# Gate and up of the last two token blocks as seven products of combined quarters, in passes of one block

## The chip, the core and the metric

The kernel runs on one core of one Trainium2 chip. The metric is the device time of one execution in microseconds (us), the median of several runs. The engines are named as in the profile: PE (matrix products; PEld is its loading of stationary operands), DVE and ACT (element-wise work; both read the PSUM banks), POOL (element-wise work on SBUF only), SP (which issues the DMAs here).

## The reference

One transformer block on 2048 tokens of width 1024, in float32: a normalisation, mixers (attention, gated linear attention, pooling), an output projection, and a gated feed-forward part. The change concerns the last part:

```python
hn = rms_norm(h, ffn_norm_g[l])
ff = jax.nn.silu(jnp.einsum('bsd,df->bsf', hn, w_gate[l])) * jnp.einsum('bsd,df->bsf', hn, w_up[l])
h = h + jnp.einsum('bsf,fd->bsd', ff, w_down[l])
```

The width inside is 2816, that is 22 tiles of 128.

## The kernel before

Tokens are handled in four blocks of 512 (`BLK`). All matrix products use float32r operands, and each number is carried as a sum of two such parts, H and L, so that a product a*b takes three matmuls, H·H, H·L and L·H. Splitting a tile is a cast to H on ACT and a subtraction on POOL or DVE for L.

The first phase (P1) projects the inputs; attention runs beside it and beside the first half of the second phase. The second phase (P2) is the output projection and the feed-forward part. It goes in passes over the weights: block 0, block 1, then blocks 2 and 3 together (`PASSES`). A pass walks through 11 groups of two hidden tiles (`GS`):

- `gate_up` makes for one hidden tile and one block the gate and the up product, each into one PSUM bank: `tile24` has 8 row tiles times 3 matmuls of 128x128 by 128x512 (L1119 to L1121).
- `ch_ff` is the side chain behind it: DVE takes both banks out with the row scale (L1136, L1138), ACT forms the sigmoid in four steps (L1140 to L1144, with one DVE step L1143 between), DVE multiplies (L1145, L1146), ACT casts to H (L1150), DVE forms L (L1151).
- `down` work: for each of the 8 output tiles one bank takes 6 matmuls (L133, from `mm`), which need H and L of both hidden tiles; DVE adds the bank to the residual (L1157).

Weights come one tile of 128x1024 at a time: SP loads it into a raw buffer, `wprep` casts it on ACT (L451) and subtracts on POOL (L452) into a buffer of `wring`. In the last pass each prepared weight serves two blocks, and there are five weight buffers and four pairs for H and L.

The order on each engine is set when the program is built: side chains are Python generators that are advanced at every `tick()` as far as their buffers allow, and a scheduler then places the instructions by its own estimate. On the chip every engine works through its own list in that order and waits at semaphores.

Of the kernel before, what the change touches and what calls it, by code (L numbers as in the profile page):

```python
# [17 lines left out]
P = 128  # L18
S = 2048
D = 1024  # L20
KT = D // P
# [19 lines left out]
class Ring:  # L41
    """Buffers handed out in turn. A buffer comes back once its last reader is in the program."""
# [13 lines left out]
class Region:  # L56
    """A phase's memory: a pool of single buffers."""
# [30 lines left out]
def body(nc, tc, V, G, ACT, PE, DMA, A, banks, dram):  # L88
    side, rside = [], []
    rate = [0.0, 0.0]  # L90
    def spawn(g):
        """Put a chain into the program as far as its buffers allow."""
        if g is not None:
            side.append(g)
            advance([g], side)
# [18 lines left out]
    def force(g):  # L114
        """Run an acquisition to its end, letting the side chains go on."""
# [19 lines left out]
    # ------------------------------------------------------------- memory  # L135
# [3 lines left out]
    # ------------------------------------------------------------- constants  # L139
# [24 lines left out]
    # ------------------------------------------------------------- DRAM scratch  # L164
# [8 lines left out]
    # ============================================================== P1  # L173
# [18 lines left out]
    class Chain:  # L192
        """Buffers of a normalisation: the two parts of the squares, ln, the result, a bank."""
# [4 lines left out]
    def meansq(sq, ones, n, c):  # L198
        """Mean of squares over the partitions of a group: a bank."""
# [10 lines left out]
    def rsq(ms, n, c):  # L210
        """-2 / sqrt(ms + eps): one Newton step on exp(-ln/2)."""
# [13 lines left out]
    # ---- normalised input of a block  # L225
# [67 lines left out]
    # ---- side chains of the projection tiles  # L293
# [81 lines left out]
    def ch_v(c, b, j, bank):  # L375
        """v of one token tile, in natural layout, split in two parts."""
# [45 lines left out]
    # ---- weights  # L422
# [11 lines left out]
    PASSES = [[0], [1], [2, 3]]  # L434
    for ps in range(len(PASSES)):
        pieces += [(("o", ps, d), None, A["w_o"][d], 0) for d in range(KT)]
        for g0 in range(0, NF, GS):
            for fi in range(g0, g0 + GS):
                pieces.append((("g", ps, fi), None, A["w_g"][fi], 0))
                pieces.append((("u", ps, fi), None, A["w_u"][fi], 0))  # L440
            for fi in range(g0, g0 + GS):
                pieces.append((("d", ps, fi), None, A["w_d"][fi], 0))
    wst = dict(dma=0, prep=0)
# [24 lines left out]
    def pump():  # L468
        """Issue the loads and splits that have room."""
        while rawring.free and wst["dma"] < len(pieces):  # L470
# [3 lines left out]
            m = KT * P if n in (0, P) else 4 * n  # L474
# [3 lines left out]
        if wring.free and wst["prep"] < wst["dma"]:  # L478
# [845 lines left out]
```

## Time and profile before

| | us |
|---|---|
| median of three runs | 2682.47 |
| lowest and highest of them | 2677.68, 2683.40 |
| span of the profiled execution, first to last instruction | 2678.9 |
| PE busy in it | 2569.5 |
| DVE busy | 1786.7 |
| ACT busy | 1179.8 |
| POOL busy | 930.5 |

The profiled execution has no time of its own beside its span. The span lies 3.6 us under the median of the runs and between their ends, so what lies around it is inside the spread of the runs. Busy times of PE count overlapping matmuls once; the time of a stretch is better read from the distance of instruction starts.

### The profile page before, as it was taken

The page shows a single profiled execution, that of the slowest core. Times are in us where ns is not written, and L with a number is a line of the kernel's source. Part 1 is how long each engine was busy: PE and PEld are TensorE (multiplying, and loading weights), DVE is VectorE, ACT ScalarE, POOL GpSimd, SP SyncE. Part 2 cuts the span into 40 slices and gives each one's busy share as a digit, 9 for nine tenths or more (in the row PEclk, how much of TensorE's full clock was granted, in tenths as well). Part 3 has the DMA queues.
Part 4 walks back from the last instruction along what each step waited for, and adds up shares of the span by engine and source line. Part 5 has one row for each costly group of instructions (what it writes and reads, how often), then busy time and mean ns, then how long its engine had stood idle before and what let it go on. Part 6 is the DMA issues. An engine that isn't in the chain of part 4 may idle for free.

```text
span 2678.9 us, 34710 instructions
## 1 busy us (share of the span) xinstructions
PE 2569.5 (96%) x12480; PEld 2118.0 (79%) x12480; DVE 1786.7 (67%) x3676; ACT 1179.8 (44%) x2205; POOL 930.5 (35%) x607
## 2 busy tenths in 40 slices
PE   7999889989999999999999999999999999999999
PEld 5887778868777877888778887787888888888887
DVE  7769886689677778778767767676364444444444
ACT  3555545357655535445544544444332222222222
POOL 4336432355733333333533333332522222222220
PEclk8999999989999999999999999999999999999999
DMA  5333645335543333346434342425211111111111
GB/s 165 122 115 112 182 144 158 114 103 182 172 122 118 118 101 112 105 124 212 122 102 117 105 121 80 138 74 178 94 44 48 48 48 47 48 48 47 48 47 63
DMA packets 145882, 284.44 MB, mean 106 GB/s; under 512 B 15292, under 2 KB 59885, under 8 KB 145709
## 3 DMA queue, kind: packets, MB, share of 16 engines
q1 hardware_dynamic: 145420, 282.20, 33.5%
q8 instruction: 98, 1.61, 0.3%
q14 instruction: 76, 0.61, 0.1%
q10 hardware_dynamic: 288, 0.02, 0.0%
HBM read 230.91 MB, written 51.25 MB: 105 GB/s over the span
## 4 chain that ended last, share of the span: by engine, by line
PE 49%; DVE 3%; ACT 1%; DMA 1%; issue 0%; POOL 0%; SPq 0%; DVEq 0%; ACTq 0%
PE bk L133 17%; PE bk L1119 10%; PE bk L1121 10%; PE bk L1120 10%; PE bk L878 1%; DVE c L1146 1%; DMA c<-mix 1%; DVE at L853 0%; DVE at L833 0%; ACT at L845 0%; DVE c L1073 0%; DMA mix<-at 0%; DVE c L1145 0%; DVE c L1138 0%; DVE c L1143 0%
## 5 line engine op out<-in xcount | busy, mean ns | idle before, releaser
L1119 PE MATMUL bk<-c,c 128*128 128x512 f32 x1136 | 450.8, 398 | 4.0 <-DVE c L217 2.4
L1120 PE MATMUL bk<-c,c 128*128 128x512 f32 x1136 | 451.0, 397 | 2.3 <-DVE c L1102 2.0
L1121 PE MATMUL bk<-c,c 128*128 128x512 f32 x1136 | 450.6, 397 | 0.7 <-POOL c L452 0.7
L452 POOL TENSOR_TENSOR c<-c,c 128x1024 fp32r<-128x1024 f32 x105 | 262.2, 2498 | 487.7 <-ACT c L451 438.9
L133 PE MATMUL bk<-p,c 128*128 128x512 f32 x1184 | 322.5, 397 | 12.2 <-DVE p L217 3.9
L133 PEld LDWEIGHTS bk<-p,c 128*128 128x128 f32 x1184 | 217.8, 189 | 59.6 <-DVE c L1138 4.8
L1119 PEld LDWEIGHTS bk<-c,c 128*128 128x128 f32 x1136 | 213.4, 188 | 53.6 <-DVE c L217 2.6
L1120 PEld LDWEIGHTS bk<-c,c 128*128 128x128 f32 x1136 | 213.6, 188 | 52.5 <-DVE c L1102 3.4
L1121 PEld LDWEIGHTS bk<-c,c 128*128 128x128 f32 x1136 | 213.5, 188 | 49.4 <-POOL c L452 0.9
L845 ACT ACTIVATE at<-at,at 128x1024 f32<-128x1024 f32 (+4 forms) x192 | 171.6, 896 | 115.3 <-DVE at L842 114.8
L833 DVE TENSOR_SCALAR_CACHE_REDUCE at<-bk 128x512 f32<-128x512 f32 (+3 forms) x304 | 153.6, 518 | 92.1 <-PE bk L133 91.4
L451 ACT CAST c<-c 128x1024 fp32r<-128x1024 f32 x105 | 110.1, 1048 | 232.8 <-PE bk L133 116.0
L1157 DVE TENSOR_TENSOR p<-p,bk 128x512 f32<-128x512 f32 x264 | 176.3, 682 | 49.7 <-PE bk L133 48.3
L998 PE MATMUL bk<-c,c 128*128 128x512 f32 x448 | 184.8, 414 | 20.1 <-ACT c L462 10.5
L452 POOL TENSOR_TENSOR c<-p,c 128x1024 fp32r<-128x1024 f32 x51 | 124.9, 2449 | 209.2 <-ACT c L451 209.2
L999 PE MATMUL bk<-c,c 128*128 128x512 f32 x448 | 184.7, 412 | 5.5 <-DVE c L250 5.5
L133 PE MATMUL bk<-c,at 128*128 128x512 f32 (+4 forms) x704 | 176.1, 349 | 11.0 <-DVE at L833 3.8
L1000 PE MATMUL bk<-c,c 128*128 128x512 f32 x448 | 183.0, 408 | 0.1
L133 PE MATMUL bk<-c,c 128*128 128x256 f32 (+1 forms) x1152 | 152.4, 286 | 7.5 <-DVE p L393 3.6
L1143 DVE SCALAR_TENSOR_TENSOR c<-c,c 128x512 f32<-128x512 f32 x88 | 81.8, 930 | 114.2 <-ACT c L1142 114.1
L133 PEld LDWEIGHTS bk<-c,c 128*128 128x128 f32 x1152 | 145.9, 190 | 11.2 <-DVE p L393 4.7
L133 PEld LDWEIGHTS bk<-c,at 128*128 128x128 f32 x704 | 121.1, 191 | 35.8 <-DVE at L833 5.4
(238 smaller groups left out, 5384.1 us busy)
## 6 DMA issues: line engine op xcount, KB each, us to landing
c<-w_g SPq DMA_DIRECT2D x44, 512.0 KB, 3.3
c<-w_u SPq DMA_DIRECT2D x44, 512.0 KB, 3.4
c<-w_d SPq DMA_DIRECT2D x44, 512.0 KB, 3.3
c<-kd SPq DMA_DIRECT2D x72, 256.0 KB, 4.6
c<-vd SPq DMA_DIRECT2D x72, 256.0 KB, 3.3
c<-xT SPq DMA_DIRECT2D x64, 256.0 KB, 3.4
at<-qd SPq DMA_DIRECT2D x64, 256.0 KB, 4.1
c<-w_e SPq DMA_DIRECT2D x28, 512.0 KB, 3.6
```

The lines of the kernel that those rows point to most:

```text
L133: PE.matmul(out, l, r, start=start and i == 0, stop=stop and i == n - 1)
L451: ACT.copy(wH, raw[:, :1024])
L452: G.tensor_tensor(wL, raw[:, :1024], f(wH), op=ALU.subtract)
L833: V.tensor_scalar(p[:, c0:c0 + far], pt[:, :far], 1.0, None, op0=ALU.mult, op1=ALU.max, accum_out=mx[:, nx:nx + 1])
L845: ACT.activation(p[:, c0:c1], p[:, c0:c1], AF.Exp, bias=nmx, accum_out=u.z[:, i, m, k:k + 1])
L998: PE.matmul(bank, wH[:, kt, :], hH[:, kt, :], start=st, stop=False)
L999: PE.matmul(bank, wH[:, kt, :], hL[:, kt, :], start=False, stop=False)
L1000: PE.matmul(bank, wL[:, kt, :], hH[:, kt, :], start=False, stop=sp)
L1119: PE.matmul(bank, wH[:, kt, :], H[:, kt, :], start=st, stop=False)
L1120: PE.matmul(bank, wH[:, kt, :], L[:, kt, :], start=False, stop=False)
L1121: PE.matmul(bank, wL[:, kt, :], H[:, kt, :], start=False, stop=sp)
L1157: V.tensor_tensor(h2[q][d], h2[q][d], bank, op=ALU.add)
```

## The change

The gate and up products of blocks 2 and 3 are made with 7 instead of 8 sub-products, in Winograd's form. For two hidden tiles at once the weight (1024 rows by 256 columns) is cut in quarters A11, A12, A21, A22, and the normalised block (1024 by 512 tokens) in quarters B11, B12, B21, B22. The seven operand pairs are A11·B11, S2·T2, S1·T1, A12·B21, S3·T3, S4·B22 and A22·T4, where S1 to S4 and T1 to T4 are sums and differences of quarters. Each is 4 row tiles times 3 matmuls, now 128x128 by 128x256 (L1351). So one unit (gate or up of two hidden tiles) has 84 matmuls of 256 columns where there were 48 of 512.

- `unit` runs the seven products into three banks z, x, y; some products are added on top of a bank whose earlier value has just been taken out (by ACT at L1357 and L1363, by DVE at L1359, L1361, L1366, L1368, L1371). The row scale is no longer applied there.
- `wpair` prepares a unit's weights: five POOL subtractions and casts of 1024 or 512 columns (L478, L479) and four DVE additions of 512 columns on the raw tiles (L495 to L498). `wprep` goes on for the rest (L526, L527).
- `ch_sig` and `ch_ffw` are `ch_ff` in two parts (L1379 to L1384; L1393, L1396, L1397).
- `tprep` makes the T operands of a block: eight normalisations, four sums and seven splits, mostly on DVE, at the end of the block before.
- Passes are of one block. The weights of gate, up and down are loaded and prepared four times instead of three. The output projections of blocks 2 and 3 stand ahead of the last group of the block before.
- Attention has to be finished in the program two groups before the end of block 1 (`until(lambda: not rside)`) instead of at its end.
- From block 2 on four more weight buffers are lent (`lend`), except in the last four groups of block 2 (`claim`).

```diff
+    def wpair(p):
+        key = pieces[p][0]
+        r0, r1 = raws.pop(p)[:, :1024], raws.pop(p + 1)[:, :1024]
...
+        def hl(w, src, o=0, n=1024):
+            ACT.copy(w[:, o:o + n], src)
+            G.tensor_tensor(w[:, 1024 + o:1024 + o + n], src, f(w[:, o:o + n]), op=ALU.subtract)
+        w = yield from wring.acq()
+        hl(w, r0)
+        put("A11", w, 0)
+        put("A12", w, 512)
...
+        hl(w, r1[:, 512:1024], o, 512)
+        put("A22", w, o)
+        a11, a12, a21, a22 = r0[:, :512], r0[:, 512:], r1[:, :512], r1[:, 512:]
+        V.tensor_tensor(a22, a21, a22, op=ALU.add)
+        V.tensor_tensor(a21, a11, a21, op=ALU.subtract)
+        V.tensor_tensor(a11, a22, a11, op=ALU.subtract)
+        V.tensor_tensor(a12, a12, a11, op=ALU.subtract)
+        w = yield from wring.acq()
+        hl(w, r0)
+        put("S2", w, 0)
+        put("S4", w, 512)
+        w = yield from wring.acq()
+        wst["busy"] = False
+        hl(w, r1)
+        put("S3", w, 0)
+        put("S1", w, 512)
...
+    def tprep(b):
+        h, rb = h2[slot(b)], acc2[slot(b)]
...
+        def hl(op, src, e):
+            H, L = TX[op]
+            ACT.copy(H, src)
+            e.tensor_tensor(L, src, f(H), op=ALU.subtract)
+            ready[("T", b, op)] = True
+        def norm(kts):
+            for kt in kts:
+                V.scalar_tensor_tensor(N[:, kt, :], h[kt], gF[:, kt:kt + 1], rb, ALU.mult, ALU.mult)
+        norm(range(4))
+        hl("B11", b11, V)
+        V.tensor_tensor(Tm["T1"], b12, b11, op=ALU.subtract)
+        norm(range(4, 8))
+        V.tensor_tensor(Tm["T2"], b22, Tm["T1"], op=ALU.subtract)
+        hl("T2", Tm["T2"], V)
...
+        hl("T4", Tm["T4"], V)
...
+        product(z, "A11", "B11", True)
+        ACT.copy(l1, z)
+        product(x, "S2", "T2", True)
+        V.tensor_tensor(r0, l1, x, op=ALU.add)
+        product(y, "S1", "T1", True)
+        V.tensor_tensor(r1, l1, y, op=ALU.add)
+        product(z, "A12", "B21", False)
+        ACT.copy(l0, z)
+        dense.rel(z_)
+        product(x, "S3", "T3", False)
+        V.tensor_tensor(r1, r1, x, op=ALU.add)
+        product(y, "S4", "B22", False)
+        V.tensor_tensor(r0, r0, y, op=ALU.add)
+        dense.rel(y_)
+        product(x, "A22", "T4", False)
+        V.tensor_tensor(l1, l1, x, op=ALU.add)
+        dense.rel(x_)
...
+            if b == 1 and g == NG - 2:
+                until(lambda: not rside)
...
+            if b in (1, 2) and g == NG - 1:
+                oproj(b + 1)
...
+            if late(b):
+                wgate_up(b, g, b)
...
+                if b in (1, 2):
+                    spawn(tprep(b + 1))
+            down(b, g, b, g == NG - 1)
```

Three places show how the lists of the engines change. In the names c, p, pp and wx are SBUF buffers and bk are PSUM banks.

DVE, before, in a group of the last pass: the chain of one hidden tile and block, and how the additions of the down banks follow.

```order
L1136 TENSOR_TENSOR c24_107<-bk2_63,pp9_15168 128x512
L1143 SCALAR_TENSOR_TENSOR c22_105<-c24_107,c22_105 128x512
L1138 TENSOR_TENSOR c23_106<-bk0_61,pp9_15168 128x512
L1145 TENSOR_TENSOR c23_106<-c23_106,c24_107 128x512
L1157 TENSOR_TENSOR p21_6283<-p21_6283,bk1_62 128x512
L1146 TENSOR_TENSOR c24_107<-c23_106,c22_105 128x512
```

DVE, now, in a middle group of block 2, during the up unit: L1361, L1366, L1368 and L1371 empty banks (bk) onto which PE's later products are added.

```order
L496 TENSOR_TENSOR pp11_14730<-c19_102,pp11_14730 128x512
L1361 TENSOR_TENSOR c22_105<-c22_105,bk7_68 128x256
L1382 SCALAR_TENSOR_TENSOR c21_104<-pp14_14733,c21_104 128x512
L498 TENSOR_TENSOR c20_103<-c20_103 128x512
L1366 TENSOR_TENSOR c22_105<-c22_105,bk1_62 128x256
L1368 TENSOR_TENSOR pp15_14734<-pp15_14734,bk7_68 128x256
L1384 TENSOR_TENSOR pp14_14733<-pp14_14733,c21_104 128x512
L1393 TENSOR_TENSOR pp13_14732<-pp15_14734,pp13_14732 128x512
L1371 TENSOR_TENSOR c22_105<-c22_105,bk1_62 128x256
L1393 TENSOR_TENSOR pp14_14733<-c22_105,pp14_14733 128x512
L1397 TENSOR_TENSOR c2_73<-pp13_14732,c2_73 128x512
```

The operations that empty a bank now stand behind operations that prepare the next group's weights (L496, L498) or the sigmoid (L1382), all of SBUF operands alone.

POOL, before: the six weights of one group of the last pass, which serve two blocks.

```order
L452 TENSOR_TENSOR pp12_15171<-p210_6292,pp12_15171 128x1024
L452 TENSOR_TENSOR c17_100<-c19_102,c17_100 128x1024
L452 TENSOR_TENSOR c18_101<-c20_103,c18_101 128x1024
L452 TENSOR_TENSOR c16_99<-p210_6292,c16_99 128x1024
L452 TENSOR_TENSOR p29_6291<-c19_102,p29_6291 128x1024
L452 TENSOR_TENSOR pp12_15171<-c20_103,pp12_15171 128x1024
```

POOL, now: one group of one block. The first two rows are its down weights, the others prepare gate and up of the next group.

```order
L527 TENSOR_TENSOR p29_6291<-c19_102,p29_6291 128x1024
L527 TENSOR_TENSOR pp10_14729<-pp11_14730,pp10_14729 128x1024
L479 TENSOR_TENSOR c17_100<-c20_103,c17_100 128x1024
L479 TENSOR_TENSOR wx2001_15417<-p210_6292,wx2001_15417 128x512
L479 TENSOR_TENSOR wx2001_15417<-pp11_14730,wx2001_15417 128x512
L479 TENSOR_TENSOR wx2002_15418<-p210_6292,wx2002_15418 128x1024
L479 TENSOR_TENSOR wx2004_15420<-c19_102,wx2004_15420 128x1024
L479 TENSOR_TENSOR c16_99<-c20_103,c16_99 128x1024
L479 TENSOR_TENSOR c18_101<-pp11_14730,c18_101 128x1024
L479 TENSOR_TENSOR wx2003_15419<-c19_102,wx2003_15419 128x1024
```

Six operations for two blocks have become ten for one.

ACT, before, between the end of a sigmoid and the cast to H that the down work waits for (L1150).

```order
L1140 ACTIVATE c22_105<-c24_107 128x512
L1141 ACTIVATE c22_105<-c22_105 128x512
L1142 ACTIVATE c22_105<-c22_105 128x512
L1144 ACTIVATE c22_105<-c22_105 128x512
L451 CAST c17_100<-c20_103 128x1024
L1150 CAST p211_6293<-c24_107 128x512
```

ACT, now, at the same place; the buffer c18 of the fifth row holds A22 of the up unit, which the unit's last product reads.

```order
L478 CAST wx2002_15418<-p210_6292 128x1024
L1363 COPY pp15_14734<-bk6_67 128x256
L478 CAST wx2004_15420<-c19_102 128x1024
L1383 ACTIVATE c21_104<-c21_104 128x512
L478 CAST c16_99<-c20_103 128x1024
L478 CAST c18_101<-pp11_14730 128x1024
L1396 CAST c2_73<-pp13_14732 128x512
L1396 CAST c2_73<-pp14_14733 128x512
```

The casts that the down work waits for (L1396) now stand behind a weight cast that can't start before the last product of the unit has ended.

## Rows read from the trace of the kernel before

**Rows 1.** The page: span, then busy time, share and count by engine.

```profile
span 2678.9 us, 34710 instructions
PE 2569.5 (96%) x12480; PEld 2118.0 (79%) x12480; DVE 1786.7 (67%) x3676; ACT 1179.8 (44%) x2205; POOL 930.5 (35%) x607
```

**Rows 2.** Timeline of DVE, last pass: start us, duration us, engine, line, operation, operands, count.

```profile
2099.93 2.70 DVE L1146 TENSOR_TENSOR c<-c,c 128x512 f32<-128x512 f32 x1
...
2166.52 2.70 DVE L1146 TENSOR_TENSOR c<-c,c 128x512 f32<-128x512 f32 x1
```

**Rows 3.** Timeline of PE in a gate product: four matmuls, the first and the fourth.

```profile
1625.63 0.40 PE L1119 MATMUL bk<-c,c 128*128 128x512 f32 x1
...
1626.33 0.40 PE L1119 MATMUL bk<-c,c 128*128 128x512 f32 x1
```

**Rows 4.** Timeline of DVE in down work: two banks of six matmuls in turn.

```profile
2062.41 0.69 DVE L1157 TENSOR_TENSOR p<-p,bk 128x512 f32<-128x512 f32 x1 [0.67 <-PE bk L133]
2063.77 0.69 DVE L1157 TENSOR_TENSOR p<-p,bk 128x512 f32<-128x512 f32 x1 [0.67 <-PE bk L133]
```

**Rows 5.** Timeline of PE in P1: unbroken runs of matmuls of 256 columns.

```profile
295.19 2.99 PE L133 MATMUL bk<-c,c 128*128 128x256 f32 x24
...
307.99 5.76 PE L133 MATMUL bk<-c,c 128*128 128x256 f32 x48
```

**Rows 6.** Groups by line and shape, PE: busy us, mean ns, idle before.

```profile
L133 PE MATMUL bk<-at,c 128*128 128x256 f32 x784 | 132.4, 288 | 0.7 <-POOL at L937 0.5
```

**Rows 7.** By line: duration ns min/median/max, first and last start; then one group by shape.

```profile
L452 POOL TENSOR_TENSOR c<-c,c x38: 2395/2408/2775, 1701.3 to 2609.0; 128x1024 fp32r<-128x1024 f32 x38
L203 POOL TENSOR_TENSOR p<-p,p x39: 1266/1292/1745, 29.3 to 1924.3; 128x512 fp32r<-128x512 f32 x39
L451 ACT CAST c<-c x38: 1032/1052/1056, 1700.1 to 2607.8; 128x1024 fp32r<-128x1024 f32 x38
L1140 ACT ACTIVATE c<-c x50: 620/632/655, 1713.1 to 2648.7; 128x512 f32<-128x512 f32 x50
L1145 DVE TENSOR_TENSOR c<-c,c x50: 681/692/2886, 1722.7 to 2654.2; 128x512 f32<-128x512 f32 x50
L1157 DVE TENSOR_TENSOR p<-p,bk x115: 668/686/689, 1700.2 to 2664.4; 128x512 f32<-128x512 f32 x115
L883 DVE TENSOR_TENSOR at<-bk,at 128x256 fp32r<-128x256 f32 x3 | 1.2, 417 | 0.2 <-ACT at L882 0.2
```

**Rows 8.** Timeline of DVE and POOL, last pass.

```profile
2055.16 2.74 POOL L452 TENSOR_TENSOR c<-c,c 128x1024 fp32r<-128x1024 f32 x1 [3.19 <-PE bk L133]
2055.61 0.69 DVE L1157 TENSOR_TENSOR p<-p,bk 128x512 f32<-128x512 f32 x1
2056.21 2.23 DVE L1146 TENSOR_TENSOR c<-c,c 128x512 f32<-128x512 f32 x1
```

**Rows 9.** Timeline of DVE and POOL in P1, both with work queued.

```profile
207.00 0.73 POOL L576 TENSOR_TENSOR gl<-gl,gl 128x256 f32<-128x256 f32 x1
207.07 1.21 DVE L352 SCALAR_TENSOR_TENSOR p<-c,c,p 64x512 f32<-64x512 f32 x1
207.70 1.59 POOL L345 TENSOR_TENSOR c<-c 128x525 f32<-128x525 f32 x1
...
208.28 1.55 DVE L463 TENSOR_TENSOR c<-c,c 128x512 fp32r<-128x512 f32 x1
```

**Rows 10.** PE's waits from 600 to 1900 us: releaser, us in total, times, longest.

```profile
PE bk L133 <- ACT p L1150: 15.7, 10, 3.2
```

**Rows 11.** Busy us by stretch, passes of block 1 and after; PEclk is the granted clock.

```profile
1637.00:1638.00 1.00, 0.45 (x1) 0.45 (x2) 0.97 (x4) 0.82 (x2) 0.00 (x0) 0.50 0.75 152
1642.00:1643.00 1.00, 1.00 (x4) 0.86 (x3) 1.00 (x5) 0.00 (x0) 0.00 (x0) 0.50 0.00 0
...
1825.00:1850.00 25.00, 21.50 (x122) 17.80 (x121) 18.32 (x30) 11.20 (x23) 4.74 (x3) 1.00 0.57 191
1850.00:1875.00 25.00, 23.17 (x99) 18.11 (x98) 11.66 (x14) 7.97 (x12) 8.79 (x5) 1.00 0.61 214
```

More of the change, by code (lines that the diff above doesn't have):

```diff
@@ L444, in body, with relop @@
+    def relop(key, op):
+        w = W2[key].pop(op)[2]
+        uses2[id(w)] -= 1
+        if uses2[id(w)] == 0 and wst["half"] is not w:
+            del uses2[id(w)]
+            wrel(w)
+        if not W2[key] and len(key) == 3:
+            W2.pop(key)
     wtile, raws, W2 = {}, {}, {}
@@ new lines, in body, with lend, claim @@
+    wx = [None]
+    def lend():
+        wx[0] = Region(tc, "wx%d" % wst["dma"], "right")
+        wst["want"] = False
+        lent.clear()
+        for _ in range(4):
+            w = wx[0].view(2048, R)
+            lent.add(id(w))
+            back.append(w)
+        wst["keep"] = list(back)
+        wring.rel(*back)
+        back.clear()
+    def claim():
+        wst["want"] = True
+        for w in [w for w in wring.free if id(w) in lent]:
+            wring.free.remove(w)
+            back.append(w)
@@ L1113, in tile24, with norm2 @@
+    def norm2(b):
+        q = slot(b)
+        hH, hL = xs[0]
+        ready[("hn", b)] = 0
+        for kt in range(KT):
+            ACT.activation(hH[:, kt, :], h2[q][kt], AF.Copy, scale=gF[:, kt:kt + 1])
+            V.scalar_tensor_tensor(hL[:, kt, :], h2[q][kt], gF[:, kt:kt + 1], f(hH[:, kt, :]), ALU.mult, ALU.subtract)
+            ready[("hn", b)] = kt + 1
+        yield from rowscale2(b)
     def tile24(bank, wH, wL, H, L, key):
@@ L1173, in gate_up, with unit, product @@
         tick()
[L1175 to L1195 removed]
+    def unit(kind, ps, g, b):
+        key = (kind, ps, g)
+        z_, x_, y_ = force(dense.acq()), force(dense.acq()), force(dense.acq())
+        z, x, y = z_[:, 0:256], x_[:, 0:256], y_[:, 0:256]
+        t0_, t1_ = force(tr2.acq()), force(tr2.acq())
+        l0, r0, l1, r1 = t0_[:, 0:256], t0_[:, 256:512], t1_[:, 0:256], t1_[:, 256:512]
+        def product(out, op, tk, start):
+            while op not in W2.get(key, {}) or not ready.get(("T", b, tk)):
+                pump()
+                tick()
+            H, L, _ = W2[key][op]
+            TH, TL = TX[tk]
+            for k in range(4):
+                for n, (l, r) in enumerate(((H, TH), (H, TL), (L, TH))):
+                    PE.matmul(out, l[:, k, :], r[:, k, :], start=start and k == 0 and n == 0, stop=k == 3 and n == 2,
+                              skip_group_check=True)
+            relop(key, op)
+            pump()
+            tick()
+        product(z, "A11", "B11", True)
[15 more added lines that the diff above has]
+        dense.rel(x_)
+        return t0_, t1_
@@ new lines, in wgate_up, with down @@
+    def wgate_up(ps, g, b):
+        gs = unit("G", ps, g, b)
+        boxes = [[], []]
+        for t_, box in zip(gs, boxes):
+            spawn(ch_sig(t_, box))
+        us = unit("U", ps, g, b)
+        for i in range(2):
+            spawn(ch_ffw(GS * g + i, b, gs[i], us[i], boxes[i]))
+    def down(ps, g, b, last):
+        grp = range(GS * g, GS * g + GS)
+        dw = [getw(("d", ps, fi)) for fi in grp]
+        for d in range(KT):
+            until(lambda: all((fi, b) in fft for fi in grp))
+            bank = force(dense.acq())
+            prs = []
+            for fi, (dH, dL, _) in zip(grp, dw):
+                fH, fL, _ = fft[(fi, b)]
+                prs += [(dH[:, d, :], fH), (dH[:, d, :], fL), (dL[:, d, :], fH)]
+            mm(bank, prs)
+            spawn(ch_down(d, b, bank, last))
+            if d % 2:
+                pump()
+            tick()
+        for fi in grp:
+            fring.rel(fft.pop((fi, b))[2])
+            relw(("d", ps, fi))
@@ L1196, in body, with oproj @@
+    def oproj(b):
+        for d in range(KT):
+            wH, wL, _ = getw(("o", b, d))
             xt = force(tr2.acq())
@@ L1198, in body @@
             bank = force(dense.acq())
[L1199 to L1201 removed]
+            tile24(bank, wH, wL, *xs[late(b)], ("mix", b))
+            relw(("o", b, d))
             spawn(ch_o(d, b, bank, xt))
```

240 lines of the change are left out of this document (155 added, 85 removed).

## The prediction

> **What bounds the kernel now.** First the busy line: PE 96% of the span, DVE 67%, POOL 35% [rows 1]. Then the last pass, which is the one the change rebuilds. The timeline of DVE repeats there every 66.59 us (two starts of L1146 [rows 2]), and a period is one group of two blocks, so one group of one block costs 33.3 us. That is PE alone: three gate or up matmuls start every 0.70 us [rows 3], so 96 of them take 22.4 us; two banks of down work, six matmuls each, are 1.36 us apart [rows 4], so 48 matmuls take 10.9 us; 22.4 + 10.9 = 33.3. PE never waits in this pass; the rest hides behind it. The 22 group-blocks of blocks 2 and 3 are 733 us of the span.
>
> **What is removed.** A unit has 84 matmuls of 256 columns for 48 of 512. A run of 48 of the narrow ones takes 2.77 us more than a run of 24 [rows 5], 0.115 us each; 5.76/48 gives 0.120 with the run-out. I take 0.117, half of the wide one's 0.233, so that a product (12 matmuls) is 1.40 us and two units are 168 x 0.117 = 19.7 us instead of 22.4. The saving is 2.7 us per group-block (2.2 to 3.1), 59 us in all (48 to 68), if PE never waits.
>
> Here a rule of the Trainium skill speaks against the change. TensorE: Matmul & The Clock Gate, section Back-to-back issue gap, gives sustained spacings of about 81 ns at 128 columns and 131 ns at 512, so that a narrow matmul costs more than its share; my estimate from that page for 256 is 98 ns, three quarters of the wide one. By it two units would take 29 us and the change would lose 7 us per group-block. The trace disagrees: its spacings are 0.115 to 0.120 against 0.233.
>
> **What is added, and where it stands.** POOL goes from 6 subtractions for two blocks to 10 for one: 8 of 1024 columns at 2.41 us and 2 of 512 at 1.29 [rows 7], 21.9 us per group-block where it was 7.2. DVE has in a group-block 16 operations on SBUF alone at 0.69 us (8 before), 10 bank evacuations of 256 columns at 0.42 and 8 of 512 at 0.69 [rows 7]: 20.8 us. ACT has about 17 us. Each sum fits under PE's 30.6 us. They don't fit together, because two engines exclude each other: L1146 has two SBUF operands, starts while POOL is in a subtraction (2055.16 to 2057.90), and ends 0.54 us after it, 2.23 us long, while L1157, which reads a bank, took its 0.69 us inside the same subtraction [rows 8]. Over all, L1145 (SBUF) reaches 2.89 us and L1157 (bank) never passes 0.69 [rows 7]. And where both have work queued they alternate: L352 waits for L576, POOL's next L345 takes 1.59 us because it waits for L352, and L463, ready on DVE at once, waits for L345 [rows 9]. So each SBUF-only DVE operation in a stretch of queued POOL work costs a POOL operation, up to 2.4 us. (The Trainium skill, SBUF, section Who interferes with whom, calls the pair of ports an exclusive lock for DVE instructions with two SBUF inputs; the trace agrees, by the 0.54 us.)
>
> In the last pass this cost nothing: nothing urgent stood behind. Now DVE's list mixes weight additions and sigmoid steps with evacuations onto which PE's next products are added. I walk one middle group through the lists, with t = 0 at its first product, a product each 1.40 us, and 0.2 us from a product's end to its reader.
> - POOL has the two down weights until 5.5, then A11/A12 of the next group (its buffer is free after product 4, cast 1.05 us [rows 7]) 6.9 to 9.3, and the A22 halves to 10.6 and 11.9. L495 needs the first half, is ready at 10.6 and gets through behind the second at 12.45. Seven operations later (L1371, L1382, L496, L495, L1359, L497, L1384; 2 x 0.42 + 5 x 0.69) DVE is at 16.7.
> - The buffer for S3/S1 is free after product 11 (15.4); cast 15.6 to 16.65; POOL asks at 16.7. DVE's next is L496, then L1361, on whose bank product 13 is added. POOL runs to 19.1, L496 to 19.7, L1361 to 20.1. Product 13, due at 16.9, starts at 20.1: **3.2 us lost**. If L496 slips in first, the same wait falls on L1382 and product 14, with the same end.
> - L1382 waits for POOL's next (to 22.1) and ends at 22.7, L498 at 23.4, L1366 at 23.8. Product 14 starts at 23.8 instead of 21.5: **2.3 us lost**.
> - It ends at 25.2. ACT's cast of A22's buffer (1.05 us) stands ahead of L1396 (0.63), so the down work could start at 27.1 at the soonest; L1393 waits for one more POOL operation until 27.7, L1396 ends at 28.4: **3.2 us lost**. Eight matmuls later the L part is needed; the second L1393 waits for S3/S1 of the next up unit until 30.5, L1397 ends at 31.2: **1.0 us lost**. The other 40 down matmuls take 9.1 us, to 40.3.
>
> So the period is 40.3 us, 30.6 + 9.7, against 33.3: +7.0. The same rows stand in 14 of the 22 group-blocks; six others have another order with the same kinds of work, and I charge them alike. The last one prepares no weights, one of the four with five buffers only some; those two I put at no change. 20 x 7.0 = **+140 us**, the saving included.
>
> The clock: before a wait of up to 3.2 us [rows 10] PE had been half idle for some us, and then it was granted 0.50, the lower level of 1.2 GHz, for six us, 1637 to 1643 [rows 11], at a cost of half of that, 3 us. A group of the walk has such a stretch from 16.9 to 31. I count it in half of the 20 groups: **+30 us** (0 to 60).
>
> The T operands: `tprep` gives DVE 8 x 0.69 and nine operations of 1024 columns at 2 x 0.69, 18 us, ahead of the last group's own chain; the last product and the first half of its down work cover some 11 us. That leaves 7 us without and some 25 us with POOL's turns. I take 13 us twice, less the 5 us that PE lost around the old pass change [rows 11]: **+21 us** (9 to 45).
>
> The end of attention: by the program's order its last 200 or so matmuls stood beside three gate-and-up pairs and stand now beside one, with 91 DVE operations or some 63 us of DVE in a stretch of PE work of about as much. Nothing if they fit, 20 us if DVE is the bound: **+8 us**. Loads (512 KB in 3.3 us, a quarter of them more) and SP's list stay far from any bound, and the moved output projections have the same matmuls: nothing.
>
> Sum: 2678.9 + 140 + 30 + 21 + 8 = 2878, and 3.6 for the median over the span: **2882 us**.
>
> **The rivals.**
> - The collisions weigh half: PE's waits are 5 us per group-block, since in the chip's timing some DVE operations find POOL between two subtractions. For it: POOL is idle from 11.9 to 16.7. Against: POOL then has four operations in a row, and DVE five of its own between them. 35.5 us a group, 20 x 2.2 + 21 + 8 = +73: 2755 us.
> - The other side: the port is free when it matters. It decides at t = 16.7: if DVE has L496, L1361, L1382 and L498 behind it before POOL's S3/S1 subtraction starts, some 2.5 us earlier than in the walk, products 13 and 14 don't wait, and only ACT's weight cast ahead of L1396 is left, 1.05 + 0.63 + 0.3 = 2.0 us, or nothing if the first hidden tile's H comes early. That is 30.6 to 32.6 us a group: -15 to -59, and with the block changes covered by down work 2624 to 2690. Against it: the two A22 halves that hold L495 until 12.45.
> - The narrow matmul costs more than its share beside other work: 132.4/784 = 0.169 us in attention [rows 6], where other matmuls stand between. 168 x 0.169 = 28.4 us, +6.0 a group, +132, without any wait: 2815 us. The run of 48 speaks against it, and it is the Trainium skill's rule of above.
> - Worse than the walk: the groups with five buffers wait for their weights, and the clock falls in every group: above 2960 us.
>
> **How the numbers follow.** Forecast 0.62, half weight 0.18, the free port 0.14, the narrow matmul 0.02, worse 0.04. The measurement can tell about 0.2% (5 us) from no change; of the free port's 0.14, 0.09 lie below that and 0.05 within. Faster 0.09, same 0.05, slower 0.86. The range from 2700 to 2960 leaves out the free port and the worst case, 0.18; the forecast's own ends (clock 0 to 60, block changes 9 to 45, attention 0 to 20, the narrow matmul 0.115 to 0.120) lie inside it.
>
> **What would show it.** L1351 at 0.117 us; the first L1316 of neighbouring groups 40 us apart; PE's waits named to DVE L1361 and L1366 and to ACT L1396; DVE's L496, L1382 and L1393 stretched to 2 or 3 us and ending about 0.54 us after an L479; a granted clock under 1 in the second half of groups. Wrong would be a group at 33 us or less, or waits for POOL's weights in place of DVE.

## The result, and the profile after

The changed kernel takes 2887.26 us (median of four runs, 2885.38 to 2891.62) against 2680.07 before: 1.0779 times as long, 95% interval 1.0755 to 1.0803. The forecast was 2882, range 2700 to 2960. The profiled execution's span grew from 2678.9 us [rows 1] to 2884.8.

The page of the changed kernel, span and busy times:

```profile
span 2884.8 us, 39094 instructions
PE 2601.4 (90%) x14064; PEld 2209.4 (77%) x14064; DVE 2051.2 (71%) x4002; ACT 1348.9 (47%) x2453; POOL 1322.5 (46%) x773
```

PE is busy 32 us longer, and that with fewer columns to go through, as part of its work ran at the lower clock (granted clock 0.70 to 0.90 in the stretches below); the other 174 us are idle time. POOL has 392 us more, DVE 265. The stretches of the changed kernel (columns: stretch, length, busy us and count of PE, PEld, DVE, ACT, POOL, granted clock, DMA share, GB/s):

```profile
1778.00:1846.00 68.00, 40.01 (x185) 32.09 (x184) 38.87 (x81) 25.83 (x49) 11.14 (x9) 0.70 0.21 70
...
1890.00:1943.00 53.00, 36.76 (x149) 29.07 (x148) 40.91 (x45) 24.11 (x31) 31.13 (x12) 0.84 0.12 41
1943.00:2341.20 398.20, 346.20 (x2162) 310.10 (x2160) 269.79 (x344) 166.65 (x245) 232.24 (x98) 0.90 0.31 96
...
2385.20:2443.20 58.00, 35.92 (x219) 32.13 (x218) 49.33 (x55) 27.89 (x38) 36.31 (x15) 0.76 0.19 65
2443.20:2884.80 441.60, 378.72 (x2377) 339.68 (x2375) 293.38 (x371) 174.14 (x257) 247.10 (x105) 0.90 0.26 81
```

In order these are the end of attention, the last group of block 1, ten groups of block 2, the last group of block 2, and block 3; the two stretches left out, 44 us each, are the output projections. Against the same work before (33.3 us a group [rows 2], the two projections and what stood around them 96 us, from 1850 to 1946) the 206 us are found again:

| part | before | after | difference |
|---|---|---|---|
| until ten groups of block 1 and attention are done | 1850 - 33.3 = 1816.7 | 1846.2 | +29.5 |
| last group of block 1, T operands of block 2 | 33.3 | 53.0 | +19.7 |
| two output projections | 96 | 88 | -8 |
| ten groups of block 2 | 333 | 398.2 | +65 |
| last group of block 2, T operands of block 3 | 33.3 | 58.0 | +24.7 |
| eleven groups of block 3 | 366.3 | 441.6 | +75.3 |

What PE waits for from the first product on (releaser, us in total, times, longest):

```profile
PE bk L133 <- ACT c L1396: 54.0, 12, 16.5
PE bk L133 <- ACT p L1396: 39.4, 11, 4.4
PE bk L133 <- DVE c L1397: 10.0, 10, 1.4
PE bk L1351 <- DVE pp L1366: 9.0, 3, 5.3
PE bk L133 <- DVE p L1397: 8.2, 7, 1.5
PE bk L1351 <- DVE c L1366: 4.0, 1, 4.0
```

Every group waits once for the cast to H (L1396), 14 of the 22 for some 4.2 us, and most wait again for L (L1397). Products waited for L1366 in only four groups of 22.

Products themselves cost what was forecast. The timeline of PE, two products of 12 matmuls:

```profile
2605.98 1.58 PE L1351 MATMUL bk<-c,p 128*128 128x256 f32 x12
2607.40 1.58 PE L1351 MATMUL bk<-c,pp 128*128 128x256 f32 x12
```

1.42 us from start to start is 0.118 us a matmul, against the 0.117 of the forecast and the 0.115 to 0.120 of [rows 5].

Now the rest of that group, DVE, POOL and PE (start us, duration us, engine, line, operation, operands):

```profile
2622.58 0.41 DVE L1361 TENSOR_TENSOR c<-c,bk 128x256 f32<-128x256 f32 x1
2622.86 3.59 POOL L479 TENSOR_TENSOR wx<-pp,wx 128x1024 fp32r<-128x1024 f32 x1 [5.03 <-ACT wx L478]
2622.91 0.68 DVE L1382 SCALAR_TENSOR_TENSOR pp<-pp,pp 128x512 f32<-128x512 f32 x1
2623.51 0.68 DVE L498 TENSOR_TENSOR c<-c 128x512 f32<-128x512 f32 x1
2624.11 0.41 DVE L1366 TENSOR_TENSOR c<-c,bk 128x256 f32<-128x256 f32 x1
...
2625.10 1.91 DVE L1384 TENSOR_TENSOR pp<-pp,pp 128x512 f32<-128x512 f32 x1
2626.41 2.80 POOL L479 TENSOR_TENSOR wx<-c,wx 128x1024 fp32r<-128x1024 f32 x1
2626.93 2.83 DVE L1393 TENSOR_TENSOR pp<-c,pp 128x512 f32<-128x512 f32 x1
2629.17 2.81 POOL L479 TENSOR_TENSOR pp<-c,pp 128x1024 fp32r<-128x1024 f32 x1
...
2630.12 2.41 DVE L1393 TENSOR_TENSOR pp<-c,pp 128x512 f32<-128x512 f32 x1
2631.94 2.81 POOL L479 TENSOR_TENSOR c<-p,c 128x1024 fp32r<-128x1024 f32 x1
2632.45 2.84 DVE L1397 TENSOR_TENSOR p<-pp,p 128x512 fp32r<-128x512 f32 x1
```

```profile
2624.58 1.68 PE L1351 MATMUL bk<-c,c 128*128 128x256 f32 x12
2630.46 3.78 PE L133 MATMUL bk<-p,c 128*128 128x512 f32 x8 [4.20 <-ACT p L1396]
2635.35 1.22 PE L133 MATMUL bk<-p,c 128*128 128x512 f32 x2 [1.11 <-DVE p L1397]
```

Four POOL subtractions and four DVE operations take turns from 2624 to 2635. The last product starts at 2624.58; the second L is ready only 10.7 us later, and until then PE can do no more than eight of the 48 down matmuls. The next group starts at 2646.73: a period of 40.75 us, where 40.3 was walked. And the clock by stretches of the same group (columns as above):

```profile
2630.00:2634.00 4.00, 3.54 (x8) 2.48 (x8) 3.97 (x3) 1.03 (x2) 4.00 (x2) 0.50 0.16 39
...
2640.00:2646.00 6.00, 6.00 (x27) 4.88 (x26) 3.49 (x6) 0.00 (x0) 0.69 (x1) 1.00 0.27 87
```

Behind the idle 4.2 us the lower level (0.50, 1.2 GHz) is granted for some nine us.

### The profile page after: what moved, and what is told of

It reads as the page before. It is cut to its first block, busy times and chain, and to the rows that moved or that the text cites. A ratio compares the mean times of both kernels' runs of the same rounds, so it can differ in the third digit from the quotient of the medians.

```text
span 2884.8 us, 39094 instructions
## 1 busy us (share of the span) xinstructions
PE 2601.4 (90%) x14064; PEld 2209.4 (77%) x14064; DVE 2051.2 (71%) x4002; ACT 1348.9 (47%) x2453; POOL 1322.5 (46%) x773
## 3 DMA queue, kind: packets, MB, share of 16 engines
q1 hardware_dynamic: 156076, 321.00, 35.9%
## 4 chain that ended last, share of the span: by engine, by line
PE 40%; DVE 13%; issue 2%; ACT 1%; POOL 1%; DMA 1%; SPq 0%; DVEq 0%; POOLq 0%; ACTq 0%
PE bk L133 16%; PE bk L1351 11%; PE bk L1278 4%; PE bk L1280 4%; PE bk L1279 4%; DVE pp L1393 2%; DVE c L1393 1%; PE bk L961 1%; DVE c L1397 1%; DVE pp L1384 1%; DVE p L1397 1%; DVE at L936 1%; DVE c L1384 1%; DVE c L1305 1%; POOL c L479 0%
## 5 line engine op out<-in xcount | busy, mean ns | idle before, releaser
L527 POOL TENSOR_TENSOR c<-c,c 128x1024 fp32r<-128x1024 f32 x91 | 226.0, 2484 | 301.6 <-ACT c L526 270.3
L133 PE MATMUL bk<-c,c 128*128 128x256 f32 (+2 forms) x1466 | 259.6, 323 | 52.9 <-ACT c L1396 39.7
L133 PEld LDWEIGHTS bk<-c,c 128*128 128x128 f32 x1466 | 214.1, 197 | 78.8 <-ACT c L1396 41.7
L1278 PE MATMUL bk<-c,c 128*128 128x512 f32 x624 | 249.3, 400 | 2.4 <-DVE c L217 2.4
L1279 PE MATMUL bk<-c,c 128*128 128x512 f32 x624 | 248.9, 399 | 2.1 <-DVE c L1268 2.1
L1280 PE MATMUL bk<-c,c 128*128 128x512 f32 x624 | 248.4, 398 | 0.0
L1351 PE MATMUL bk<-c,wx 128*128 128x256 f32 x1824 | 232.9, 283 | 9.5 <-DVE c L1366 4.0
L1351 PEld LDWEIGHTS bk<-c,wx 128*128 128x128 f32 x1824 | 223.6, 189 | 12.3 <-DVE c L1359 4.5
L1081 PE MATMUL bk<-c,c 128*128 128x512 f32 x448 | 184.3, 413 | 19.0 <-ACT c L537 9.4
L1082 PE MATMUL bk<-c,c 128*128 128x512 f32 x448 | 184.2, 411 | 5.1 <-DVE c L250 5.1
L1083 PE MATMUL bk<-c,c 128*128 128x512 f32 x448 | 182.2, 407 | 1.4 <-DVE c L538 1.4
L527 POOL TENSOR_TENSOR c<-p,c 128x1024 fp32r<-128x1024 f32 x45 | 110.5, 2456 | 145.6 <-ACT c L526 145.6
L526 ACT CAST c<-c 128x1024 fp32r<-128x1024 f32 x91 | 95.3, 1047 | 167.2 <-PE bk L133 80.2
L133 PE MATMUL bk<-p,p 128*128 128x512 f32 x384 | 127.3, 451 | 41.9 <-ACT p L1396 15.3
L1351 PE MATMUL bk<-c,c 128*128 128x256 f32 x1128 | 149.1, 285 | 4.6 <-DVE pp L1366 3.7
```

What stands on the lines that cost most here:

```text
L133: PE.matmul(out, l, r, start=start and i == 0, stop=stop and i == n - 1)
L527: G.tensor_tensor(wL, raw[:, :1024], f(wH), op=ALU.subtract)
L1081: PE.matmul(bank, wH[:, kt, :], hH[:, kt, :], start=st, stop=False)
L1082: PE.matmul(bank, wH[:, kt, :], hL[:, kt, :], start=False, stop=False)
L1083: PE.matmul(bank, wL[:, kt, :], hH[:, kt, :], start=False, stop=sp)
L1278: PE.matmul(bank, wH[:, kt, :], H[:, kt, :], start=st, stop=False)
```

## The experiments

Each kernel but the changed one was run once, beside the kernel before (2677 to 2683 us). That kernel's runs lie 9 us apart (2674.5 to 2683.4), so a difference of less than that between two single runs shows nothing. The table's last column is block 3, from its first product to the end, over its 11 groups; its first group is in it.

| kernel | us | us per group in block 3 |
|---|---|---|
| before | 2677 to 2683 | 33.3 |
| e1_single | 2698.5 | |
| the changed kernel | 2887.3 | 40.1 |
| e2_shortpool | 2745.6 | 33.2 |
| e3_filler | 2929.7 | 41.7 |
| e10_filler_y | 2899.0 | 40.8 |
| e12_halves | 2873.4 | 38.7 |
| e8_dve_l | 2844.0 | 38.3 |
| e7_tail | 2870.1 | 40.1 |
| e4_pipe | 2785.9 | 34.4 |
| e6_pipe_dve | 2768.9 | 34.6 |
| e13_pipe_halves | 2764.6 | 33.8 |
| e9_changes | 2760.8 | 36.5 |
| e11_pipe_shortpool | 2703.1 | 31.6 |

**Passes of one block, plain products** (e1_single; edit of the kernel before):

```diff
-    PASSES = [[0], [1], [2, 3]]
+    PASSES = [[0], [1], [2], [3]]
...
-        if len(bl) == 2:
+        if ps == 2:
```

> The kernel before, eight plain products, with blocks 2 and 3 in passes of their own; nothing else is changed. If the loss is the product form's (theory: PE waits between the up unit and the down work, and its clock falls behind that wait), the plain groups stay near 33.3 us each: 22 x 0.7 us of waits as in block 1 (15.7 us in ten waits there), some clock behind them, and a second block change: 2695 to 2740 us. If the passes of one block are the loss by themselves (each group's chain is exposed because no second block's gate and up work covers it), the groups take 38 us and more and the time is 2790 to 2850 us.

2698.5 us, 21 above its neighbour. So the passes are a tenth of the loss. PE's waits in blocks 2 and 3:

```profile
PE bk L133 <- ACT pp L1150: 4.1, 10, 2.5
PE bk L133 <- ACT p L1150: 2.9, 9, 1.4
```

The plain chain is exposed here too, with 19 such waits in 22 groups, and they cost a third of a us per group. POOL has six subtractions per group here instead of ten; that this is the reason is not shown by this run, but by the next.

**POOL's subtractions cut short** (e2_shortpool):

```diff
-            G.tensor_tensor(w[:, 1024 + o:1024 + o + n], src, f(w[:, o:o + n]), op=ALU.subtract)
+            G.tensor_tensor(w[:, 1024 + o:1024 + o + n // 8], src[:, :n // 8], f(w[:, o:o + n // 8]), op=ALU.subtract)
```

> The changed kernel, but POOL forms only an eighth of the columns of L in the ten-per-group subtractions that prepare gate and up (the rest of L keeps old numbers; the lent buffers are cleared once). Every wait stays. Theory of the shared port: L1384, L1393 and L1397 on DVE fall from 1.9 to 2.8 us to 0.7, the down work starts 2 us behind the last product instead of 4.2, L1397 is no wait any more, a middle group takes 33 us if the clock then holds and 36 if it falls as before: 2715 to 2800 us. Theory of the bare chain (bank, DVE, ACT, DVE one behind the other, whatever the port): groups stay at 39 us or more, 2850 us or more.

The edit reaches the eight of POOL's ten subtractions of a group that prepare gate and up; the two of the down weights stay whole. 2745.6 us, 142 under the changed kernel, inside the port's range. The same place in a group (timeline of all engines):

```profile
2594.66 0.69 DVE L1394 TENSOR_TENSOR c<-c,c 128x512 f32<-128x512 f32 x1
...
2597.12 2.11 PE L133 MATMUL bk<-p,c 128*128 128x512 f32 x8 [1.54 <-ACT p L1397]
2597.68 0.68 DVE L1398 TENSOR_TENSOR p<-c,p 128x512 fp32r<-128x512 f32 x1
```

(All lines below L1250 are one higher here.) The chain's operations are back at 0.7 us, PE waits 1.54 us instead of 4.2 and 1.1, and block 3 runs at a granted clock of 1.00. DVE has the same operations, in nearly the same order, so it is POOL's holding of the port that stretches the chain. Without it a group of the product form takes 33.2 us on average (32.7 in the middle of the block), the time of a plain one: most of the 2.7 us of saving is used up by a chain that now lies open.

**Idle matmuls against the clock** (e3_filler, e10_filler_y). Both put matmuls that nobody reads behind the last product, the first 30 into the bank of that product, the second 36 into one that is free sooner (edit of the second):

```diff
+NDUM = 36
...
+        product(x, "A22", "T4", False)
+        if kind == "U" and g < NG - 1:
+            TH = TX["B11"][0]
+            for n in range(NDUM):
+                PE.matmul(y, TH[:, n % 4, 0:128], TH[:, n % 4, :], start=n == 0, stop=n == NDUM - 1)
         dense.rel(y_)
-        product(x, "A22", "T4", False)
```

> The changed kernel with 30 idle matmuls (128x128 by 128x256, 0.117 us each, 3.5 us) into the up unit's last bank once it has been emptied, so that PE works through most of the 4.2 us in front of the down work. No result depends on them. If the clock's fall to 0.50 follows from that wait, it stays at 1.00, the down work takes 12 us instead of 16.3 and a group 36.5 instead of 40.75: 19 x -4.3 = -82, about 2800 us. If the clock falls for another reason, or the waits alone count, nothing is gained: 2880 to 2900 us.

> The changed kernel with 36 idle matmuls (128x128 by 128x256, 4.2 us) right behind the up unit's last product, into the bank that DVE emptied one product earlier, so that they need not wait for the last bank as the first filler did. No result depends on them, and the down work's own wait of 4.2 us covers them. If the granted clock falls because of that wait, it stays at 1.00 through the down work, which then takes 12 us instead of 16.3: 18 to 20 groups x -4.3, about 2800 to 2810 us. If the clock's fall has another cause, 2880 to 2905 us.

Neither gained anything: 2929.7 us, above both cases of the first, and 2899.0 us, in the second case of the second, though not for its reason. In the first the idle matmuls had themselves to wait up to 3.9 us for the emptying of the last bank, which stands behind stretched DVE operations. The second did what was meant, and shows why it doesn't help (PE, one group, then its stretches, columns as above):

```profile
2592.92 4.48 PE L1374 MATMUL bk<-c 128*128 128x256 f32 x36
2597.36 1.43 PE L134 MATMUL bk<-c,c 128*128 128x512 f32 x5
2602.28 0.73 PE L134 MATMUL bk<-c,c 128*128 128x512 f32 x2 [3.48 <-DVE c L1402]
```

```profile
2593.00:2598.00 5.00, 5.00 (x40) 4.74 (x39) 4.96 (x4) 1.67 (x2) 5.00 (x3) 1.00 0.37 105
2598.00:2602.00 4.00, 0.80 (x4) 0.31 (x2) 4.00 (x2) 0.62 (x1) 3.67 (x2) 1.00 0.46 128
...
2604.00:2606.00 2.00, 2.00 (x7) 1.52 (x6) 0.03 (x1) 1.04 (x1) 0.76 (x1) 0.50 0.66 246
```

The clock held through the filler, as expected. But then the down matmuls that need only H were done at once, the wait for the second L (L1402 here, L1397 in the changed kernel) grew from 1.1 to 3.5 us, and the clock fell behind that wait instead. So the low clock before L1397 costs nothing, since PE would otherwise wait; only what is left of it behind L1397 does. A group's end hangs on when the second L is ready.

**Turns of one operation?** (e12_halves):

```diff
-            G.tensor_tensor(w[:, 1024 + o:1024 + o + n], src, f(w[:, o:o + n]), op=ALU.subtract)
+            for c in range(0, n, 512):
+                G.tensor_tensor(w[:, 1024 + o + c:1536 + o + c], src[:, c:c + 512], f(w[:, o + c:o + c + 512]), op=ALU.subtract)
```

> The changed kernel with each POOL subtraction of 1024 columns in the gate and up weights made as two of 512 (1.29 us each instead of 2.41): the same numbers, a little more POOL time, the same order on every other engine. If the two engines take turns one operation each, a DVE operation now lets half as much POOL work pass: the four stretched ones between the last product and the second L1397 take some 1.7 us each instead of 2.5, the second L part comes 3.4 us earlier, and with less of the low clock a group takes 35.5 to 37.3 us instead of 40.75: 2780 to 2815 us. If what counts is the total time that POOL holds the port (or its whole queue goes first), nothing is gained: 2870 to 2890 us.

2873.4 us, inside the other theory's range. Yet the turns are seen, and shorter (timeline of DVE and POOL; x2 are two subtractions in one row; lines below L480 are one higher than in the changed kernel):

```profile
2582.52 3.41 POOL L480 TENSOR_TENSOR wx<-c,wx 128x512 fp32r<-128x512 f32 x2
...
2584.72 1.76 DVE L1394 TENSOR_TENSOR c<-c,c 128x512 f32<-128x512 f32 x1
2585.89 3.42 POOL L480 TENSOR_TENSOR pp<-c,pp 128x512 fp32r<-128x512 f32 x2
...
2589.28 3.40 POOL L480 TENSOR_TENSOR wx<-pp,wx 128x512 fp32r<-128x512 f32 x2
2589.79 1.75 DVE L1398 TENSOR_TENSOR c<-c,c 128x512 fp32r<-128x512 f32 x1
```

The stretched DVE operations now take 1.1 to 1.8 us instead of 1.9 to 2.8. But there are twice as many POOL operations to take turns with, so twice as many DVE operations are caught: in this group eight, the first two of which (L1382 and L498 of the changed kernel) stand ahead of the bank of product 14, and that product waits 1.84 us. The second L is ready at 2591.54, 28.8 us into the group instead of 29.3: 0.5 us earlier, where 3.4 was expected. This group gained more than that, as its clock stayed at 1.00; on average a group of block 3 gained 1.4 us. Both theories were half right: the turns are one for one, and DVE is held for as long as POOL's queue lasts (11.9 us of four subtractions in the changed kernel, from 2622.86 on; 13.1 us of eight halves here, from 2579.59 on).

**Two subtractions given to DVE** (e8_dve_l; S2/S4 and S3/S1 of each unit):

```diff
-        def hl(w, src, o=0, n=1024):
+        def hl(w, src, o=0, n=1024, e=G):
...
-            G.tensor_tensor(w[:, 1024 + o:1024 + o + n], src, f(w[:, o:o + n]), op=ALU.subtract)
+            e.tensor_tensor(w[:, 1024 + o:1024 + o + n], src, f(w[:, o:o + n]), op=ALU.subtract)
...
-        hl(w, r0)
+        hl(w, r0, e=V)
         put("S2", w, 0)
...
-        hl(w, r1)
+        hl(w, r1, e=V)
         put("S3", w, 0)
```

> The changed kernel, with two of the five POOL subtractions of a unit (S2/S4 and S3/S1, 1024 columns each) given to DVE; same numbers, same places in the program. POOL's 21.9 us of a group become 12.3, DVE gets 4 x 1.3 us more of SBUF work (26 us of 30.6). If the stretched DVE operations between the last product and the down work are POOL's doing, they fall to 0.7 us here too, and a group takes 33 to 36 us: 2725 to 2785 us. If DVE is late because its list is long, whoever holds the port, the longer list makes it worse: 2870 us or more.

(A unit has four POOL subtractions, three of 1024 columns and one of 512, not five as said above: eight in a group beside the two of the down weights, 176 of L479 in the trace.) 2844.0 us, between the two: the chain was only partly relieved (a group 38.3 us where 33 to 36 was expected). In block 3 PE still waits up to 3.2 us for L1396; in the timeline the subtractions that moved, 1.21 us each, stand between the two L1393 and ahead of L1397.

**The down work one gate unit later** (e4_pipe; the core of its edit), and the same with the edits of e8_dve_l (e6_pipe_dve), e12_halves (e13_pipe_halves) and e2_shortpool (e11_pipe_shortpool):

```diff
         for t_, box in zip(gs, boxes):
             spawn(ch_sig(t_, box))
+        if g:
+            down(ps, g - 1, b, False)
         us = unit("U", ps, g, b)
```

> The changed kernel with the down work of group g-1 moved in between the gate unit and the up unit of group g (its weights are loaded in that order too), so that a group's sigmoid chain has a whole gate unit of PE work to hide behind. If the exposed chain and the clock behind it are the whole loss: no waits at L1396 and L1397, the clock at 1.00, a group at PE's 30.6 to 31.5 us: 20 x -9.5, about 2695 us. If the port is the bound behind it: POOL's 21.9 us and 16 DVE operations on SBUF alone at 0.69 us exclude each other, 32.9 us, and with the chance order of the two 33 to 36 us a group: 2735 to 2800 us. If the waits only move to the products: 2850 us or more.

> Both together: the down work one gate unit later, and S2/S4 and S3/S1 subtracted on DVE. Port time of a group falls from 32.9 us to 12.3 on POOL and 16.4 on DVE, 28.7, under PE's 30.6. If the port was what kept the shifted kernel above PE's time, a group takes 31 to 32 us instead of about 33 and the whole 2735 to 2765 us; if not, it stays at 2785 or goes above.

> The shifted kernel (down work one gate unit later) with POOL's gate and up subtractions in halves of 512 columns. All work is done. By turns of one operation the waits of PE for L1362 and L1369 (emptying of banks behind a stretched DVE operation) halve: groups of 33 us become 31.5 to 32, 2750 to 2765 us. If the total port time of 33 us is the bound, it stays at 2775 to 2790 us.

> The shifted kernel (down work one gate unit later) with POOL forming only an eighth of L's columns in the gate and up weights (the rest of L keeps old numbers). If what kept the shifted kernel's groups at about 33 us is the port, they now take PE's 30.6 to 31.2 us, and the time is 2784 - 20 x 2 = 2735 to 2750 us: all that is left above the kernel before is then attention's end and the two block changes. If DVE's own list (weight additions ahead of the emptying of banks) is what holds PE there, it stays at 2765 us or more.

The shift alone brings 100 us (2785.9; the port's case). A chain that has a gate unit to hide behind costs no wait of 4.2 us in each group any more, and the low clock is nearly gone with it (0.99 in block 3). S2/S4 and S3/S1 on DVE brought 17 us in all but none in block 3 (34.6 us a group where 31 to 32 was expected), and 2768.9 lies between the two cases: e6_pipe_dve missed. Halves brought 21, and 2764.6 is just inside what turns of one operation promised, but not by their way: a group of block 3 takes 33.8 us where 31.5 to 32 was expected. With POOL cut short the shifted kernel reaches PE's own time: over most of block 3 PE's waits fall from some 15 us to 0.5, and clock and busy share in a stretch of it are (columns as above)

```profile
2400.00:2500.00 100.00, 100.00 (x707) 93.52 (x707) 63.19 (x111) 53.98 (x78) 30.91 (x32) 1.00 0.33 105
```

and at 2703.1 us it came out under its range. So it is POOL that keeps the shifted groups above PE's time. That bounds the idea: even with 31.6 us a group, and with work left out, the kernel is 20 us slower than before; what is left to account for it is the end of attention and the two block changes.

**The end of attention and the changes** (e7_tail on the changed kernel, e9_changes on e6_pipe_dve). The core of the edit:

```diff
-            if b == 1 and g == NG - 2:
+            if b == 1 and g == NG - 1:
                 until(lambda: not rside)
...
-            if b in (1, 2) and g == NG - 1:
+
+            def project():
                 oproj(b + 1)
...
+            if b == 2 and g == NG - 1:
+                project()
...
                 if b == 1:
                     fring.rel(X[1][:, 2048:3072], X[1][:, 3072:4096])
+                    project()
                 if b in (1, 2):
                     spawn(tprep(b + 1))
...
+                    down(b, g - 1, b, False)
```

(The last line stands for blocks 1 and 2 in e9_changes, for block 1 alone in e7_tail.)

> The changed kernel with only the end of block 1 rearranged: attention has to be finished before the last group instead of before the one ahead of it, the output projection of block 2 stands behind the last group's gate and up work, and the last two groups' down work behind that. The groups of blocks 2 and 3 and the second block change stay. By the traces attention's end costs 29 us against the kernel before and the first change 20. If PE lacked other work there (the matmuls of attention's last chain are few and wait for each other), 25 to 40 us come back: 2845 to 2860 us. If it is DVE's load there, nothing: 2875 us or more.

> The kernel with both, and the block changes rearranged: attention has to be finished one group later (before the last group of block 1), the output projection of block 2 stands behind that group's gate and up work, and the down work of the last two groups of blocks 1 and 2 stands together behind the T operands' preparation. By the comparison of the traces the attention's end costs 29 us and the two changes 37 us against the kernel before. If PE merely lacked other work there, some 40 to 50 us come back: 2690 to 2725 us. If DVE's list (T operands, mixed rows) is the bound there, 15 us or less: 2730 to 2755 us.

e7_tail gained 17 us, between its two cases. The first product came 27 us earlier (1915.7 instead of 1943.0), so PE did lack work there; but 12 us were given back in the ten groups that follow, since the first of them then waited for T operands:

```profile
PE bk L1355 <- ACT c L1217: 7.0, 1, 7.0
PE bk L1355 <- DVE c L1218: 3.7, 2, 3.3
```

(L1217 and L1218 are the casts and subtractions of `tprep`.) e9_changes gained 8 us, no more than runs of one kernel differ by, and 2760.8 lies in neither of its ranges. Its first products came 33 us earlier than those of e6_pipe_dve, and its groups were slower (36.5 us in block 3), with a wait for the cast to H in most. Why these groups fell into a worse order is open. No version of the product form here that does all the work beats the kernel before; the nearest are some 80 us above it.

## Why the prediction was right, point by point

- **The narrow matmul**: 0.118 us, so the saving per group-block was there. By the sustained spacings of the Trainium skill (TensorE: Matmul & The Clock Gate, section Back-to-back issue gap) a narrow one would have cost more than its share; the trace disagrees, 0.118 against half of 0.233.
- **The port**: the mechanism was right, and shown by e2_shortpool. Of the stretches named, L1393 is seen (2.83 us), and it ends 0.55 us after POOL's subtraction (2629.76 and 2629.21), as the sign named with 0.54 asked. In most groups L496 and L1382 were not stretched. The Trainium skill (SBUF — State Buffer, section Who interferes with whom) says that the order of issue decides which of the two engines blocks. The turns agree; the start of POOL's first subtraction doesn't: it is recorded at 2622.86, L1382 at 2622.91, and yet L1382 and L498 went first in 0.68 us each, and POOL took 3.59.
- **The waits at products 13 and 14** (3.2 and 2.3 us) were mis-placed. They hung on who goes first at t = 16.7, and POOL did ask at 16.9; but in most groups DVE slipped in with two operations. That was the condition of the rival of the free port, and its 30.6 to 32.6 us did not follow, because POOL's remaining queue then met the next four DVE operations. One group of block 3 went the walk's way, in its variant with L1382 and product 14 (DVE, POOL and PE):

```profile
2743.20 2.38 POOL L479 TENSOR_TENSOR wx<-p,wx 128x1024 fp32r<-128x1024 f32 x1 [4.78 <-ACT wx L478]
2743.50 2.63 DVE L1382 SCALAR_TENSOR_TENSOR pp<-c,pp 128x512 f32<-128x512 f32 x1
2745.53 2.81 POOL L479 TENSOR_TENSOR wx<-c,wx 128x1024 fp32r<-128x1024 f32 x1
2746.06 2.83 DVE L498 TENSOR_TENSOR c<-c 128x512 f32<-128x512 f32 x1
...
2749.28 2.93 PE L1351 MATMUL bk<-c,wx 128*128 128x256 f32 x12 [3.96 <-DVE c L1366]
```

  There POOL was recorded 0.30 us ahead of L1382 instead of 0.05; product 14 waited 3.96 us, and the group took 39.8 us (2726.3 to 2766.1). So the order changes the place of the wait and hardly the period: the same four POOL subtractions stand on the way to the second L either way.
- **The down start and L1397**: walked at 28.4 and 31.2 us of the group, measured at 24.5 (2630.46) and 29.3 (2635.29). The waits named, L1396 and L1397, were right in kind: 4.2 and 1.1 us for 3.2 and 1.0.
- **The clock** was mis-sized: 3 us in half of the groups were charged. It falls in nearly every group, and costs the 40 matmuls behind L1397 2.3 us (11.4 us from 2635.35 to 2646.73 instead of 9.1); what it slows before L1397 is covered, as e10_filler_y shows. The 1.9 us by which the walk was late and this clock nearly cancel: that 40.3 us walked without any clock meet 40.75 measured with it is luck.
- **Sums**: 170 us were charged for 20 groups with their clock; 21 groups lost 140, 6.7 each instead of 8.5, as steady groups hold their clock loss in the 40.75, and two of those with five weight buffers took only 35.7 and 35.9 us (2230.32 to 2301.84). Longer waits there for weights, a part of the worst rival, did not come.
- **T operands and changes**: +21 charged, about +36 measured (19.7 + 24.7 - 8, the last group of block 2 in it). PE waited 12.4 us for L1309 at the first and 16.5 for L1396 at the second: DVE's `tprep` stands ahead of the last group's own chain, as said, and these waits lie between the two cases of 7 and 25 us, near the 13 charged. What was left out is a second wait at each (3.8 us for L1297, 5.3 for L1366) and the clock, 0.84 and 0.76 there.
- **The end of attention**: mis-sized, +8 (0 to 20) for +29.5. What was costed was DVE's load, but DVE was busy for only 38.9 of these 68 us. What decided was order: PE waited some 11 us between the few matmuls of attention's last chain, each of which waits for the step before, and then 17 us for the down work of the tenth group (DVE, PE):

```profile
1818.27 1.37 DVE L1156 TENSOR_TENSOR mx<-c,mx 128x512 fp32r<-128x512 f32 x2 [1.84 <-DMA mix<-at]
1819.56 0.68 DVE L1295 TENSOR_TENSOR c<-bk,p 128x512 f32<-128x512 f32 x1
...
1833.07 6.95 PE L133 MATMUL bk<-p,pp 128*128 128x512 f32 x20 [17.16 <-ACT p L1309]
```

  That group's chain begins with L1295, which stands in DVE's list behind the mixed rows of block 2 (L1156), and these wait for a DMA behind attention's last step; more rows of L1156 stand between the steps of its sigmoid. With other PE work moved there (e7_tail), the first product comes 27 us earlier.

So the direction, the loss per group and the kind of wait came out by the mechanism. That the total came out within 5 us is luck: the groups lost 30 us less than charged, and the changes and attention some 36 more.

## What to carry to other kernels

A saving on the busiest engine has to be set against what the new preparation does to the engines that feed it: here 2.7 us of PE per group were bought with 15 us of POOL, and POOL's subtractions and DVE's operations with two SBUF operands took turns instead of running side by side. Look for the chain that PE waits for at the end of each group, count the POOL operations that can be queued while it runs, and charge DVE one of them for each of its operations. Moving the consumer one stage later hid this chain better (100 us) than making the competing operations shorter (14 us) or moving them (43 us); and price the edges of a loop (its first and last group, the end of what ran beside it) as carefully as its middle, since here they alone, some 66 us, outweighed the 59 us of saving that were forecast.

## What the runs showed of the hardware

- With work queued on both, DVE and POOL took turns operation by operation: a DVE operation of 0.68 us with two SBUF operands took up to 2.9 us against POOL's 1024 columns and up to 1.8 against 512. A bank operation (L1371, 0.41 us) was never held: the longest of its 44 took 0.42 us.
- A POOL operation that came out of idle was not always served in the order of the recorded starts: recorded 0.03 to 0.06 us ahead of DVE's L1382, it went behind two DVE operations (seven groups of block 3); recorded 0.30 us ahead, it went first (one group).
- PE's idle time of 4.2 us in the changed kernel, or of 3.5 in e10_filler_y, was followed by a granted clock of 0.50 in every group that had one. Shorter waits were not followed by the same each time: behind three of 1.84, 2.02 and 2.27 us within ten us (e12_halves, the group from 2562.8) the clock stayed at 1.00, and behind 1.89, 2.01 and 2.28 us in the next group it fell (0.87 on average from 2625 to 2633).
